# One expert weight piece loaded earlier, normalized rows written contiguously, and filler matmuls ahead of a mixer, in a two-block mixture-of-experts kernel

## The chip, the cores and the metric

The kernel runs on one core of one Trainium2 chip. The metric is the device time of one execution in microseconds (us); less is better. TensorE is called PE, its weight loads PEld, VectorE DVE, ScalarE ACT, GpSimd POOL, and SyncE, whose queue issues nearly all weight transfers, SP.

## What is computed

256 tokens of width 1024 in float32 pass two blocks. The first has two layers, each a mixer (three kinds of attention over one projection) and a mixture of 16 experts, with a layer norm behind each of the two. The second block has another mixer and again 16 experts. Cut to the part around the change:

```python
def first_block(x, ...):
    h = layer_norm(x, ln_in_g, ln_in_b)
    for l in range(DEPTH):                                      # DEPTH = 2
        mix = mixer_sublayer(h, ...)
        h = layer_norm(DEEPNORM_ALPHA * h + mix, ln1_g[l], ln1_b[l])
        ffn = grouped_moe(h, router_w, router_bias, exp_w_gate[l], exp_w_up[l], exp_w_down[l])
        h = layer_norm(DEEPNORM_ALPHA * h + ffn, ln2_g[l], ln2_b[l])
    return h

def grouped_moe(h, ...):                                        # two experts of one group for each token
    ...
    for e in range(N_EXPERTS):                                  # 16
        a = jax.nn.silu(h @ w_gate[e]) * (h @ w_up[e])          # 1024 -> 512
        y = y + dense_gates[:, e:e + 1] * (a @ w_down[e])       # 512 -> 1024
    return y
```

Each expert has 6 MB of weights, so each of the three expert stages reads 96 MB.

## The kernel before

The program is one straight sequence for each engine, with the order of the work written out by hand. Tokens lie in two tiles of 128 partitions (i = 0, 1).

**Experts.** `moe()` treats the 16 experts as 8 pairs. `gather(q)` (L986) brings the tokens of four experts into groups of 64 slots with one-hot matmuls. For each pair, `expand(pr, 0)` and `expand(pr, 1)` (L1026) do gate and up, 32 matmuls each, into one PSUM tile apiece; each of these matmuls needs one 512-wide row of one expert's weight half. `shrink(pr - 1)` (L1073) does the down product of the pair before, `slots` and `turn` (L1042, L1057) prepare the next step, and `scatter(pr - 1)` (L1099, L1101) adds the result into `yacc`. Behind the first gather, PE and the other engines load a flag and branch over `overflow` (L1127, L1128), code for experts with more than 64 tokens which isn't entered with these inputs.

**Weight stream.** `moe_loads` makes a list of 96 jobs of 1 MB for each expert stage: pair 0 gate, pair 0 up, pair 1 gate, pair 1 up, pair 0 down, pair 2 gate and so on, four jobs each (two halves by two experts). A letter in `MOE_SEQ` says from which pool of tiles a job takes its place; job 3, the second half of expert 1's gate in pair 0, has the letter q, four quarter pieces of 256 KB in tiles of the pool "m2" (5 slots), which the mixer before uses for its softmax work. `wload` (L114) issues a job on SP's queue, in order, so a transfer whose tile isn't free yet holds all behind it. `LATE = (3, 21), (3, 20)` takes job 3 out of the list and puts it back at position 21 in the first block's stages and 20 in the second block's: it is issued behind jobs 16 to 19 (pair 0's down) and two or one of pair 2's gate. The mixer issues the first jobs, and `load(MOE_FIRST[blk])` (L1014) those up to 22 or 21. Tiles that the mixer frees late, such as those that PE reads for pada, and the DMA of an ada row, hold some of these jobs.

**From experts to mixer.** The last pair's `scatter` calls `last(i, n)` for each token tile and half: DVE takes statistics of the half row, and after the second half `ln_scale` (L277, on POOL) gives scale and shift and `ln_rest` applies them through `ln_apply` and `evac` (L132 on ACT, L141 on DVE), two instructions for each token tile. They write `xn2` as [token, 8, 128] with the feature index split so that an instruction reads `yacc` with a step of 32 bytes. `to_T` (L291) then transposes each 128x128 block of `xn2` on PE, with the block as the stationary operand, and evacuates it as `h2T` with gain and shift, four pieces on ACT and four on DVE for each tile. Between the two, PE does the `pada` products of an adaptive scale (L1244), 16 matmuls. `warm(n)` (L121) issues n matmuls on a constant that nobody reads.

Of the kernel before, what the change touches and what calls it, by code (L numbers as in the profile page):

```python
# [21 lines left out]
D = 1024  # L22
P = 128
# [8 lines left out]
AHEAD = 6  # L32
KMC, FLG = (1, 3), 3
EXT, EXT2 = 0, 0
LATE = (3, 21), (3, 20)
PARTS = {"r": "rr", "x": "r4", "y": "44", "z": "422", "q": "2222"}
GATHER = (1, 3, 5)
MOE_FIRST = 22, 21
# [2 lines left out]
LNE, ADA_AT, ADA_1 = "p", "ak0", (2, 3)  # L41
# [6 lines left out]
class Net:  # L48
# [1790 lines left out]
    def run(self):  # L1839
        A, nc = self.A, self.nc  # L1840
        self.loads()
        c = self.c
        W = self.mixer_loads(0)
        nc.scalar.preload_act_table_set("silu_and_others")
        hT, hp = self.ln_in()
        for l in range(2):
            nc.gpsimd.tensor_scalar(c["qg", l], c["qg", l], 96 ** -0.5, None, op0=ALU.mult)
        self.wstream([(n, W[n]) for n in WSTREAM])
        self.wahead(2)
        tr = iter(())  # L1850
        for l in range(2):
            fill = self.ada(ADA_MX[l], W["ada"])
            h1 = []
            g, b = c["ln1_g", l], c["ln1_b", l]
            pr, parts = [], []

            def mid(xn):

                h1.append(self.big([P, 8, S], "h1T"))
                self.to_T(xn[:, 0], h1[0], g, b, 0)  # L1860
                self.warm(2)
                parts.append(self.parts())
                self.split_hi(xn, parts[0], 0)
                pr.append(self.ps("prt", "o"))
                self.router_mm(h1[0], c["rw"], 16, pr[0], 0)
                self.warm(3)

            We = lambda e: (A["exp_w_gate"][l, e], A["exp_w_up"][l, e], A["exp_w_down"][l, e])
            loads = self.moe_loads(We, MOE_SEQ[0], LATE[0])
            xn = self.mixer(l, hT, hp, W, fill, mid, tr, loads[0])  # L1870
            h1T, pr, parts = h1[0], pr[0], parts[0]
            self.split_lo(xn, parts, 0)
            self.split_hi(xn, parts, 1)
            self.to_T(xn[:, 1], h1T, g, b, 1)
            yacc = self.big([P, 2, D], "yacc")
            self.to_tok(h1T, yacc[:, 0, :], 0, ALPHA, "a", "s")
            self.warm(2)
            self.router_mm(h1T, c["rw"], 16, pr, 1)
            self.split_lo(xn, parts, 1)
            self.dbg(f"h1T{l}", h1T)  # L1880
            mask, gates = self.router1(pr)

            self.to_tok(h1T, yacc[:, 1, :], 1, ALPHA, "a", "s")
            next(fill, None)
            self.warm(4)
            xn2, sts = [], []

            def last(i, n):
                if i == 0 and n == 0:
                    xn2.append(self.big([P, 2, 8, P], "xn2"))  # L1890
                if n == 0:
                    sts.append(self.stats())
                nc.vector.bn_stats(sts[i][:, n, :], yacc[:, i, n * 512:(n + 1) * 512])
                if n == 1:
                    self.ln_rest(yacc, i, self.ln_scale(sts[i], LNE), xn2[0], "aa" if i == 0 else "av")

            self.moe(0, loads, parts, g, b, mask, gates, We, yacc, None, last, fill)
            Wa = self.ada_loads(ADA_TR[l:l + 1])
            W = self.mixer_loads(1) if l == 0 else self.mixer2_loads()
            fill = self.ada(ADA_TR[l:l + 1], Wa, "s", l == 0)  # L1900
            hT = self.big([P, 8, S], "h2T")
            next(fill)
            if l == 0:
                hp = self.hparts()
                self.wstream([(n, W[n]) for n in WSTREAM])
                for i in range(2):
                    self.to_T(xn2[0][:, i], hT, c["ln2_g", l], c["ln2_b", l], i, "ta"[i])
                next(fill)
                for i in range(2):
                    self.hl_tile(hT, hp, i)  # L1910
                tr = fill
                self.wahead(2)
            else:
                sq = self.big([P, 8, S], "sq2")
                self.wstream([(n, W[n]) for n, _ in WIN2_TILES])
                for i in range(2):
                    self.to_T(xn2[0][:, i], hT, c["ln2_g", l], c["ln2_b", l], i, "ta"[i])
                    self.square2(hT, sq, i)
                hp = self.hparts()
                self.wahead(2)  # L1920
                self.rms2(hT, sq, hp, fill)
        We = lambda e: (A["w1_2"][0, e], A["w3_2"][0, e], A["w2_2"][0, e])
        loads = self.moe_loads(We, MOE_SEQ[1], LATE[1])
        xt, parts, h3T, pr, g2b = self.mixer2(hT, hp, W, loads[0])
        self.dbg("x1", xt)
        self.dbg("h3T", h3T)
        mask, gates = self.router2(pr)

        def last(i, n):
            s = slice(n * 512, (n + 1) * 512)  # L1930
            nc.sync.dma_start(self.out[0, i * P:(i + 1) * P, s], xt[:, i, s])

        self.moe(1, loads, parts, self.mcol[:, 4, :], self.mcol[:, 3, :], mask, gates, We, xt, g2b, last)


# [148 lines left out]
```

## Time and profile before

| | us |
|---|---|
| median of 3 runs | 1238.4 (1237.06 to 1243.48) |
| profiled execution | 1240.28 |
| its span in the trace | 1238.6 |
| PE busy | 1161.9 (94%) |
| mean granted clock of PE | 0.976 |

The three expert stages run from about 191 to 404 (layer 0), 579 to 790 (layer 1) and 1024 to the end (second block), with the mixers between. Times in rows are in us from the start of the span unless ns is said. A row of a timeline gives a group of like instructions on one engine: start, length from the first to the last, engine, line of the kernel, operation, output and inputs, shapes and count, and in brackets the idle time of the engine ahead of it and what ended that. A table by stretches gives, for each stretch, how long each engine was busy, the granted clock of PE (1.00 is its full 2.4 GHz), the busy share of the 16 DMA engines and what they moved.

### The profile page before, as it was taken

Reading aid. Unit: us, or ns where it says so; the run is one execution under the profiler, and the core shown is the slowest. Engines: PE = TensorE matmul, PEld = TensorE weight load, DVE = VectorE, ACT = ScalarE, POOL = GpSimd, SP = SyncE. Lnnn points to the kernel's source line nnn. Section 1 sums busy time; section 2 is a strip of 40 time slices with the busy share of each in tenths; the row PEclk is TensorE's granted clock in tenths of the full one; section 3 lists DMA queues with packets and bytes.
Section 4 is the critical chain, followed back from the end, with each engine's and each line's share of the span. In section 5 each row is a group of like instructions: output and inputs, shape, how many; then the busy total and the mean of one; then the engine's idle time right before and its main releaser. Section 6 shows DMA issues by size and latency. Waiting matters only on the chain. (4 is left out here: it accounts for less than half of the span.)

```text
span 1238.6 us, 16671 instructions
## 1 busy us (share of the span) xinstructions
PE 1161.9 (94%) x6366; PEld 673.6 (54%) x6366; DVE 517.1 (42%) x1135; ACT 381.4 (31%) x799; POOL 245.6 (20%) x356
## 2 busy tenths in 40 slices
PE   5999897999999799997999999899899989999997
PEld 4887453434344688645344343489898453434432
DVE  6565351212232756535023221565985360223323
ACT  5545341111111655424011011465464340101100
POOL 4655200000000356320000000132473200000000
PEclk9999898999999999999999999889899998999999
DMA  9814958999999964677999999984354267999995
GB/s 383 338 65 186 399 185 327 408 404 413 414 416 414 419 256 138 248 263 295 378 405 415 413 415 414 418 321 154 114 194 172 102 263 312 415 414 416 415 417 232
DMA packets 77947, 395.46 MB, mean 319 GB/s; under 512 B 7936, under 2 KB 9592, under 8 KB 49440
## 3 DMA queue, kind: packets, MB, share of 16 engines
q1 hardware_dynamic: 73488, 384.66, 78.2%
q0 software_dynamic: 2608, 7.73, 1.6%
q10 hardware_dynamic: 1760, 1.89, 0.5%
q8 instruction: 53, 0.87, 0.3%
q14 instruction: 38, 0.31, 0.1%
HBM read 389.41 MB, written 6.51 MB: 320 GB/s over the span
## 5 line engine op out<-in xcount | busy, mean ns | idle before, releaser
L1026 PE MATMUL pz<-we,xT 128*64 128x512 f32 x1536 | 343.9, 604 | 19.8 <-DMA we<-in_exp_w_gate 12.3
L1026 PEld LDWEIGHTS pz<-we,xT 128*64 128x64 f32 x1536 | 110.8, 139 | 239.6 <-issue 217.8
L1073 PE MATMUL py<-wd,aT 128*64 128x512 f32 x768 | 171.1, 593 | 0.9 <-DMA wd<-in_w 0.9
L1035 DVE TENSOR_TENSOR act<-sil,pz 128x512 f32<-128x512 f32 x24 | 16.5, 688 | 327.8 <-PE pz L1026 302.8
L1050 POOL TENSOR_SCALAR m_ge<-m_s 64x1 f32<-64x1 f32 x48 | 11.9, 247 | 586.5 <-DVE m_s L1045 339.9
L1073 PEld LDWEIGHTS py<-wd,aT 128*64 128x64 f32 x768 | 56.6, 137 | 110.2 <-issue 105.6
L1030 ACT ACTIVATE sil<-pz 128x512 f32<-128x512 f32 x24 | 14.3, 597 | 217.8 <-PE pz L1026 217.8
L1079 ACT ACTIVATE yh<-py,m_ge 128x512 fp32r<-128x512 f32 x32 | 22.0, 688 | 187.6 <-PE py L1073 187.6
L1080 DVE SCALAR_TENSOR_TENSOR yl<-py,m_ge,yh 128x512 fp32r<-128x512 f32 x32 | 24.0, 751 | 96.3 <-ACT yh L1079 96.3
L541 PE MATMUL pout<-w_o,oT 128*128 128x512 f32 x128 | 58.2, 602 | 0.0
L986 PE MATMUL pg<-G,xhi 128*128 128x256 f32 x192 | 47.8, 290 | 2.0 <-DVE G L975 2.0
L448 POOL TENSOR_SCALAR E<-E,r 128x128 f32<-128x128 f32 x40 | 31.6, 791 | 77.4 <-DVE r L444 77.2
L986 PE MATMUL pg<-G,xlo 128*128 128x256 f32 x192 | 46.7, 283 | 0.0
L1085 ACT ACTIVATE yh<-yf 128x512 fp32r<-128x512 f32 x16 | 10.1, 631 | 104.0 <-DVE yf L1084 104.0
L1099 PE MATMUL psc<-yh,GT 128*128 128x512 f32 x96 | 39.3, 410 | 1.1 <-ACT yh L1085 0.8
L1101 DVE TENSOR_TENSOR yacc<-yacc,psc 128x512 f32<-128x512 f32 x64 | 40.1, 680 | 0.0
L1099 PE MATMUL psc<-yl,GT 128*128 128x512 f32 x96 | 38.5, 401 | 1.3 <-DVE yl L1080 0.6
L541 PEld LDWEIGHTS pout<-w_o,oT 128*128 128x128 f32 x128 | 23.8, 194 | 26.0 <-issue 25.6
L986 PEld LDWEIGHTS pg<-G,xhi 128*128 128x128 f32 x192 | 36.7, 191 | 2.4 <-issue 1.6
L986 PEld LDWEIGHTS pg<-G,xlo 128*128 128x128 f32 x192 | 36.8, 191 | 0.0
L442 ACT ACTIVATE E<-s,nm 128x128 f32<-128x128 f32 (+1 forms) x48 | 20.2, 421 | 47.9 <-DVE nm L441 45.6
L1244 PE MATMUL pada<-wa,cz 128*32 128x512 f32 x192 | 24.2, 618 | 8.4 <-DVE yacc L1101 4.5
(512 smaller groups left out, 2122.4 us busy)
## 6 DMA issues: line engine op xcount, KB each, us to landing
wd<-in_exp_w_down SPq DMA_DIRECT2D x58, 1024.0 KB, 16.3
we<-in_exp_w_up SPq DMA_DIRECT2D x54, 1024.0 KB, 13.1
we<-in_w SPq DMA_DIRECT2D x52, 1024.0 KB, 15.0
we<-in_exp_w_gate SPq DMA_DIRECT2D x48, 1024.0 KB, 11.7
wd<-in_w SPq DMA_DIRECT2D x29, 1024.0 KB, 15.3
wa<-in_p_ada SPq DMA_DIRECT2D x24, 1024.0 KB, 15.2
we<-in_exp_w_gate SPq DMA_DIRECT2D x28, 512.0 KB, 13.7
we<-in_w SPq DMA_DIRECT2D x22, 512.0 KB, 14.8
```

The source lines that it names most:

```text
L442: nc.scalar.activation(E[:, s], sc[:, s], AF.Exp, bias=nm[:, i:i + 1], accum_out=sm[:, i:i + 1])
L448: self.nc.gpsimd.tensor_scalar(E[:, 0:P], E[:, 0:P], r[:, 0:1], None, op0=ALU.mult)
L541: self.nc.tensor.matmul(acc, oT[:, cc, i * P:(i + 1) * P], w[cc][:, n * 512:(n + 1) * 512], start=(cc == 0), stop=(cc == 7), skip_group_ch ...
L986: nc.tensor.matmul(pg[:, :256], part[:, i, k, :], Gq[q][:, i].rearrange("p e s -> p (e s)"), start=(n == 0), stop=(n == 3))
L1026: nc.tensor.matmul(pz[64 * e:64 * e + 64, :], x[:, k, o + 64 * e:o + 64 * e + 64], w[e][k], start=(k == 0), stop=(k == 7), skip_group_chec ...
L1035: nc.vector.tensor_mul(a, st[pr].pop("sil"), pz)
L1073: nc.tensor.matmul(py[n][64 * e:64 * e + 64, :], aT[:, f, 64 * e:64 * e + 64], w[e][f][:, n * 512:(n + 1) * 512], start=(f == 0), stop=(f ...
L1079: nc.scalar.activation(yh[:, s], py[n], AF.Copy, scale=ge)
L1080: nc.vector.scalar_tensor_tensor(yl[:, s], py[n], ge, yh[:, s].bitcast(F32), op0=ALU.mult, op1=ALU.subtract)
L1099: nc.tensor.matmul(pt, GT[:, i * P:(i + 1) * P], y[:, s], start=(j == 0), stop=(j == 1), skip_group_check=True)
L1101: nc.vector.tensor_tensor(yacc[:, i, s], yacc[:, i, s], pt, op=ALU.add)
L1244: nc.tensor.matmul(pa[32 * k:32 * k + 32, :], c["cz"][:, 4 * k4 + k:4 * k4 + k + 1].to_broadcast([P, 32]), w[:, k, :], start=(k4 == 0), st ...
```

## The change

Three edits. Job 3 is put back at position 16 of the list in all three expert stages, that is right behind job 16 and ahead of jobs 17 to 21 (17 to 20 in the second block). `xn2` becomes [token, tile, 1024] and is written contiguously, tile 0 by ACT, tile 1 by ACT and DVE; `to_T` gets a rearranged view of it, so that the transposes' stationary operand is read with a step of 32 bytes. And `warm(9)` and `warm(4)` are put around the first `next(fill)` behind the experts (the pada matmuls), in both layers.

```diff
-LATE = (3, 21), (3, 20)
+LATE = (3, 16), (3, 16)
...
             def last(i, n):
                 if i == 0 and n == 0:
-                    xn2.append(self.big([P, 2, 8, P], "xn2"))
+                    xn2.append(self.big([P, 2, D], "xn2"))
...
                 if n == 1:
-                    self.ln_rest(yacc, i, self.ln_scale(sts[i], LNE), xn2[0], "aa" if i == 0 else "av")
+                    rs, nm = self.ln_scale(sts[i], LNE)
+                    for j in range(2):
+                        s = slice(j * 512, (j + 1) * 512)
+                        self.evac(xn2[0][:, i, s], yacc[:, i, s], rs, nm, "a" if i == 0 else "av"[j])
...
             hT = self.big([P, 8, S], "h2T")
+            self.warm(9, "t")
             next(fill)
+            self.warm(4, "t")
             if l == 0:
...
                 for i in range(2):
-                    self.to_T(xn2[0][:, i], hT, c["ln2_g", l], c["ln2_b", l], i, "ta"[i])
+                    self.to_T(xn2[0][:, i].rearrange("t (q k) -> t k q", k=8), hT, c["ln2_g", l], c["ln2_b", l], i, "ta"[i])
...
                 for i in range(2):
-                    self.to_T(xn2[0][:, i], hT, c["ln2_g", l], c["ln2_b", l], i, "ta"[i])
+                    self.to_T(xn2[0][:, i].rearrange("t (q k) -> t k q", k=8), hT, c["ln2_g", l], c["ln2_b", l], i, "ta"[i])
                     self.square2(hT, sq, i)
```

## Rows read from the trace of the kernel before

**Rows 1.** Table by stretches: length, engines' busy time, PEclk, DMA share, GB/s
```profile
176.20:191.00 14.80, 13.78 (x100) 11.14 (x99) 9.33 (x32) 9.36 (x15) 2.11 (x4) 0.88 0.77 287
191.00:230.00 39.00, 31.99 (x137) 10.70 (x137) 3.24 (x12) 3.45 (x5) 0.87 (x3) 0.91 0.96 365
230.00:386.00 156.00, 156.00 (x783) 66.79 (x780) 39.48 (x76) 23.18 (x37) 3.60 (x13) 1.00 1.02 413
564.00:578.50 14.50, 12.51 (x100) 9.58 (x99) 10.55 (x38) 10.21 (x17) 1.48 (x3) 1.00 0.79 294
578.50:614.00 35.50, 28.96 (x124) 9.99 (x126) 2.39 (x9) 2.26 (x4) 0.88 (x3) 0.90 0.96 376
1024.00:1035.00 11.00, 11.00 (x40) 3.72 (x42) 0.00 (x0) 0.60 (x1) 0.00 (x0) 0.74 0.46 157
```

**Rows 2.** DMA issues at 365.8: transfer, count, size, us to landing
```profile
wd<-in_exp_w_down SPq DMA_DIRECT2D x1, 1024.0 KB, 20.1
```

**Rows 3.** Timeline of PE, pair 6's down product in layer 0
```profile
383.73 7.59 PE L1073 MATMUL py<-wd,aT 128*64 128x512 f32 x32
```

**Rows 4.** Timeline of PE, pair 0 in layers 0 and 1, an undisturbed pair
```profile
191.59 4.50 PE L1026 MATMUL pz<-we,xT 128*64 128x512 f32 x18 [0.35 <-ACTq L1128]
202.47 12.79 PE L1026 MATMUL pz<-we,xT 128*64 128x512 f32 x46 [6.38 <-DMA we<-in_exp_w_gate]
578.78 4.48 PE L1026 MATMUL pz<-we,xT 128*64 128x512 f32 x18 [1.23 <-PEq L1128]
589.22 12.27 PE L1026 MATMUL pz<-we,xT 128*64 128x512 f32 x46 [5.97 <-DMA we<-in_exp_w_gate]
1197.16 13.95 PE L1026 MATMUL pz<-we,xT 128*64 128x512 f32 x64
```

**Rows 5.** Timeline of SP's queue around layer 0's first expert pair
```profile
176.61 14.29 SPq L114 DMA_DIRECT2D wd<-in_exp_w_down  x4
191.00 6.18 SPq L114 DMA_DIRECT2D we<-in_exp_w_gate  x8
```

**Rows 6.** Waits of SP's queue, 170 to 226: releaser, total us, times, longest
```profile
SPq L114 <- PE pada L1244: 6.4, 1, 6.4
SPq L114 <- DMA ada<-wa: 6.1, 1, 6.1
```

**Rows 7.** Timeline of PE, head of the second block's experts
```profile
1010.49 2.57 PE L121 MATMUL warm<-onesb 128*128 128x512 bf16 x11
1023.91 16.81 PE L1026 MATMUL pz<-we,xT 128*64 128x512 f32 x64 [5.52 <-issue]
```

**Rows 8.** DMA queues, 609.2 to 1022.6: packets, MB, share
```profile
q8 instruction: 18, 0.29, 0.3%
```

**Rows 9.** Table by stretches, 609 to 1021.4 and the last gather
```profile
608.97:1021.36 412.39, 392.99 (x2286) 251.68 (x2282) 195.84 (x405) 147.17 (x284) 86.61 (x101) 0.98 0.75 295
1013.80:1018.50 4.70, 4.20 (x32) 3.95 (x32) 2.60 (x8) 2.24 (x4) 0.50 (x1) 1.00 1.03 410
```

**Rows 10.** DMA queues, 1021.3 to 1022.6: packets, MB, share
```profile
q8 instruction: 1, 0.02, 5.3%
```

**Rows 11.** Timelines of PE and ACT behind the experts of layers 0 and 1
```profile
406.49 1.92 PE L1244 MATMUL pada<-wa,cz 128*32 128x512 f32 x16 [2.23 <-DVE yacc L1101]
406.88 2.55 ACT L132 ACTIVATE xn<-yacc,nm,rs 128x512 f32<-128x512 f32 x2 [4.90 <-POOL nm L277]
409.49 1.09 PE L291 MATMUL pt<-pk,xn 128*128 128x128 f32 x8 [1.07 <-ACT xn L132]
409.86 1.33 ACT L132 ACTIVATE xn<-yacc,nm,rs 128x512 f32<-128x512 f32 x1 [0.42 <-POOL nm L277]
411.09 2.88 ACT L132 ACTIVATE h2T<-pt,pk 128x128 f32<-128x128 f32 x8
799.88 5.99 PE L1327 MATMUL pss<-sq,ones 128*128 128x128 f32 x32 [0.76 <-ACT sq L1315]
```

**Rows 12.** The page, costliest groups: busy us, mean ns, idle before; contiguous write on ACT
```profile
L1085 ACT ACTIVATE yh<-yf 128x512 fp32r<-128x512 f32 x16 | 10.1, 631 | 104.0 <-DVE yf L1084 104.0
```

## Prediction of the time after the change

> **What bounds the kernel now.** The page gives TensorE (PE) as busy nearly throughout, which doesn't say what a saved microsecond of PE is worth, so I read the table by stretches first, then the last jobs of the stages, then their heads. In the steady part of the first expert stage (230 to 386) PE is busy without a gap at full clock, and the DMA engines move 413 GB/s with their share at its top [rows 1]: the two run level. Which of them ends the stage is seen at its last jobs. The down half of pair 6 is issued at 365.8 and lands 20.1 us later, at 385.9 [rows 2], while pair 6's down product, which uses it, starts at 383.73 and takes 7.59 us [rows 3]; the run is stretched because it caught up with its weights. So PE has little slack before the weight stream, and **an expert stage ends earlier only by the DMA time that is recovered**, not by all the PE time.
>
> At the head of a stage both have holes. In layers 0 and 1 PE does 18 of the 64 matmuls of pair 0's gate and up, then waits 6.38 and 5.97 us for the gate's fourth piece; the other 46 take 12.79 and 12.27 us, where an undisturbed pair takes 13.95 for 64 (0.218 each, 10.0 for 46): the granted clock fell behind the wait (means of 0.91 and 0.90 there [rows 1]) and cost 2.8 and 2.2 us more [rows 4]. The piece is issued late: SP's queue issues four down jobs from 176.61 to 190.9, held by pada for 6.4 us and by an ada row for 6.1 us, and only behind them the gate's transfers from 191.00 [rows 5, 6]. The DMA engines have spare time meanwhile. At 413 GB/s, 176.2 to 191 moved 287 (14.8 x (1 - 287/413) = 4.5 us idle) and 191 to 230 moved 365 (4.5 us); in layer 1, 564 to 578.5 moved 294 (4.2) and 578.5 to 614 moved 376 (3.2) [rows 1].
>
> **Edit 1, the piece ahead of the down jobs.** It adds and removes no byte; four 256 KB transfers pass jobs 17 to 21 (17 to 20 in the second block) on SP's queue. Issuing them costs SP under 0.8 us each (eight transfers in 6.18 us, waits included [rows 5]), and SP waits 6.4 us for pada right behind them anyway [rows 6]. Their tiles' slots were last used by the mixer's softmax work and ought to be free by then. In layer 0 the piece then goes at about 177 and lands before 190, the 6.4 us wait goes, and the clock should hold. PE's part: 6.4 + 2.8 = 9.2 us, in layer 1 6.0 + 2.2 = 8.2, and perhaps the 1.23 us at the branch. DMA's part: 1.05 MB more move in the first stretch, 1.05/0.413 = 2.5 us of its 4.5. Two us stay there, since the down jobs behind it still wait for pada and the ada row, which don't move [rows 6]. Of the 4.5 behind 191, pair 0's earlier end frees the next buffers about 9 us sooner, and 2.7 to 4.5 come back. Together 5.2 to 7.0; I take **6.0**. Layer 1 likewise 2.5 + 2.0 to 3.2 = 4.5 to 5.7; I take **5.3**. The rest of PE's saved 9 us should turn into small waits for down tiles near the stage's end.
>
> The second block differs. Its fourth piece isn't what PE waits for: PE idles 5.52 us until 1023.91 with nothing named as releaser ("issue"), and then runs all 64 matmuls in 16.81 us [rows 7], 2.9 us over 13.95, in a stretch with mean clock 0.74 where DMA fell to 157 GB/s (11 x (1 - 157/413) = **6.8 us idle**) [rows 1]. The idle PE lies just behind the gather and the branch over the overflow code. Instruction packets on queue q8 are rare: 18 between 609 and 1022.6 [rows 8], for 2286 matmuls and 2282 weight loads [rows 9], 254 instructions to a packet. The last of them moves inside this idle time, after 1021.3 [rows 10]. I read it as PE waiting for the code behind the branch. The fillers of edit 3 put 26 matmuls and weight loads, 52 instructions, ahead of this place (26 for each layer), so the place where a packet is wanted falls 52 instructions earlier; the gather ahead of the branch is 64 instructions in 4.2 us [rows 9], so the packet is wanted up to 52/64 x 4.2 = 3.4 us earlier, and PE would start near 1020. Only then could the fourth piece, issued behind the down jobs here too, have bound, and edit 1 has moved it away. If so PE gains about 3.9 us at the start and 2.9 of clock, and DMA's hole closes: 6.0 to 6.8, I take **6.0**. If the packet comes as late as before, **0**. Nothing in the trace of before tells me at which instruction a packet is asked for, so both ends stay in the range.
>
> The Trainium skill, "Runtime: NRT & Kernel Launch", section "Instruction fetch mechanics", says that engines' code streams in 16 KiB blocks of 256 instructions and that a taken branch to a target that isn't loaded waits for a DMA fetch. The 254 instructions to a packet agree with it; that the wait depends on where the branch falls in a block follows from the rule, but no run of before shows it moved.
>
> **Edit 2, normalized rows written as they lie.** Each of four rows per layer (two token tiles by two halves) is written contiguously. ACT's row with the 32-byte step took 1.33 and 1.27 us [rows 11]; a contiguous 128x512 on ACT took 0.631 [rows 12]. Tile 0's two rows end 1.3 us earlier, tile 1's 0.7. PE's chain: transposes of tile 0 at 409.49 waited 1.07 for them, those of tile 1 follow the 1.33 us row, and then eight evacuations of 2.88 us set the mixer's start [rows 11]. These aren't shortened, and they begin with tile 1's row done: gain 0.6 in layer 0. In layer 1 the same 0.5, with a clock that falls there too: 32 matmuls of the square sums take 5.99 us, 0.19 each [rows 11]. If the new fillers hold the clock, up to 2.1 more; together I take **1.5** in layer 1, **0.6** in layer 0.
>
> In exchange the transposes take their stationary operand with the 32-byte step. No PE operand of before has that step, so its price is bounded: 0 by PE's own pace (8 in 1.09 us [rows 11]), and at the other end ACT's pace at this step, 1.33 us/512 = 2.6 ns a column, 0.33 us for 128, 2.7 us for 8: 1.6 more per tile. Tile 0's has 1.1 us in hand while ACT writes tile 1's row, tile 1's has none: 2.1 us per layer, 4.2 in all at most. A gain is excluded, since the same 128 columns are read. I take 0, because the evacuations behind them, at 0.36 us a piece, are still slower than ACT's pace per transpose (0.33), so the chain goes on at its old rate. The Trainium skill, "SBUF — State Buffer", section "Door 1: The DMA port swizzle", says that accesses that go to a new 16-byte line each time pay a penalty. ACT's 1.33 against 0.631 agrees; by it the transposes would be slower, which is rival D.
>
> **Edit 3, fillers.** 9 + 4 matmuls of 0.234 us (11 took 2.57) [rows 7]. Nine are 2.1 us against the 2.23 us in which PE waits ahead of pada; four are 0.9 and end by about 409.4, where the transposes start at 409.49 [rows 11]. Cost 0 while that cover stands; up to 0.5 us per layer as edit 2 lets the transposes start 1 us sooner, which is in the 0.6 above.
>
> **The sum.** 6.0 + 5.3 + 6.0 + 0.6 + 1.5 = 19.4 us. The profiled execution took 1240.28 us (span 1238.6), 1.9 above the median 1238.4. From it 1220.9, from the median 1219.0; I say 1220.
>
> **Rivals and chances.** About 0.5% (6.2 us) is what a measurement of this kernel tells from no change.
> A, as summed, 1220: 0.42.
> B, the packet of the second block comes as late as before: without the 6.0, 1226: 0.23. For it: the delay may be the branch's, not the block's.
> C, PE's time passes whole (buffers free earlier carry the stream on): 9.2 + 8.2 + 6.8 + 2.1 + 1.2 = 27.5, 1211: 0.10. Against it: the shrink that caught up [rows 3].
> D, the strided transposes cost their 4.2: 1224 with A, 1230 with B: 0.10. For it: ACT's two rows [rows 11, 12]; against it: ACT's evacuations set the pace.
> E, waits for the late down tiles become long enough for the clock to fall again, as behind the waits for the piece [rows 4], 2 to 3 us per layer on top of B: 1231: 0.06.
> F, slower: the piece's tile slots aren't free at 177. SP issues in order, so 17 to 21 then wait behind the piece. From the point at which the slots come free later than the transfers issued by then have landed (I put it at 184), the engines run dry, and where they come only at 191, up to 5 us per layer: 10, less the 2 us of edit 2: 1247: 0.05. For it: the trace shows that the slots were free at 191, not at 177.
> G, nothing gained, the stages end by the same last transfers: 1237: 0.04.
> Faster by over 0.5%: A to D and most of E, 0.88; within: the rest of E, G and a mild F, 0.08; slower: F, 0.04. The range leaves out F, G and the far end of C: 1212 to 1231.
>
> **What would show it.** Right: pair 0's 64 matmuls in one run of about 14 us in layers 0 and 1, SP issuing the piece ahead of 178; over 380 GB/s from 176 to 230 but for the pada wait; a PE start in the second block within 2 us of the branch, and no fall to 157 GB/s. Wrong: a wait of several us at pair 6's down product, an "issue" wait of 5 us at the second block's start, transposes above 1.1 us per 8 in both transitions, or down jobs issued later than before.

## The result: 12 to 14 us faster, and the profile after

The changed kernel takes 1225.47 us (median of 4 runs, 1222.1 to 1226.33) against 1237.83 us of the kernel before (4 runs). The ratio is 0.9883, with a 95% interval of 0.9852 to 0.9913. Run again beside the later experiments it took 1226.28 us (6 runs, 1223.07 to 1227.08) against 1240.66, a ratio of 0.9879 (0.9854 to 0.9904). The forecast was 1220 us with a range of 1212 to 1231: the direction and the range hold, the gain is two thirds to four fifths of the 18.4 us forecast.

The profiled execution took 1224.84 us, span 1223.2 (before: 1240.28 and 1238.6). Where its 15.4 us come from is read off PE's timeline. A stage is counted from the first gather matmul's start to the last scatter's end, the mixers lie between; negative numbers are time saved.

| stretch | before | after | difference | forecast |
|---|---|---|---|---|
| up to the first gather | 187.1 | 185.6 | -1.6 | 0 |
| experts of layer 0 | 217.1 | 211.6 | -5.5 | -6.0 |
| mixer of layer 1 | 169.2 | 170.3 | +1.1 | -0.6 |
| experts of layer 1 | 216.9 | 212.9 | -4.0 | -5.3 |
| second block's mixer | 223.8 | 222.6 | -1.3 | -1.5 |
| experts of the second block, tail included | 224.4 | 220.2 | -4.2 | -6.0 |

In the profile of the repeat the three stages came out the same (-5.6, -4.0, -4.0); the first line did not (-0.1). No edit lies ahead of that point, so it isn't part of the change: of that time PE had its lower clock for 10.2 us in the first profile of the changed kernel, and for 17.1 us in the profile of before and in that of the repeat.

The heads of the stages, from PE's timeline of the changed kernel (start, length, engine, line, operation, tiles, shapes, count, idle time ahead and its releaser), to be held against [rows 4, 7]:

```profile
192.42 13.95 PE L1026 MATMUL pz<-we,xT 128*64 128x512 f32 x64 [2.74 <-PEq L1128]
573.70 15.60 PE L1026 MATMUL pz<-we,xT 128*64 128x512 f32 x64 [2.10 <-PEq L1128]
1010.21 15.65 PE L1026 MATMUL pz<-we,xT 128*64 128x512 f32 x64 [3.04 <-PEq L1128]
```

The waits of 6.38 and 5.97 us for the gate's piece are gone, and pair 0's matmuls stand in one run. In layer 0 they take the 13.95 us of an undisturbed pair; in layer 1 and the second block the granted clock fell in them (15.60 and 15.65 us). What's new is the bracket: PE now waits 2.74 us in layer 0 and 2.10 in layer 1 at its own branch, where it had 0.35 and 1.23.

SP's queue, to be held against [rows 5]: the four quarter pieces go out at 175.72, the down jobs behind them are held as before.

```profile
175.19 0.42 SPq L114 DMA_DIRECT2D wd<-in_exp_w_down  x1
175.72 2.23 SPq L114 DMA_DIRECT2D we<-in_exp_w_gate  x4
178.04 12.28 SPq L114 DMA_DIRECT2D wd<-in_exp_w_down  x3
```

The table by stretches (length, busy time of PE, PEld, DVE, ACT, POOL, granted clock, DMA share, GB/s) is to be held against [rows 1]; the stretches are the same pieces of work, moved with it:

```profile
174.60:189.40 14.80, 13.77 (x101) 10.87 (x99) 9.52 (x32) 9.50 (x16) 2.12 (x4) 0.90 0.93 337
189.40:221.00 31.60, 28.56 (x137) 10.91 (x137) 3.24 (x12) 3.48 (x5) 0.87 (x3) 1.00 0.99 395
558.00:572.50 14.50, 12.57 (x101) 9.57 (x99) 10.57 (x37) 10.23 (x17) 1.48 (x3) 1.00 0.92 338
572.50:602.00 29.50, 27.99 (x126) 10.13 (x128) 2.41 (x9) 2.32 (x4) 0.88 (x3) 0.94 1.00 401
1010.00:1021.00 11.00, 10.79 (x44) 4.28 (x46) 0.52 (x4) 1.13 (x2) 0.25 (x1) 0.84 0.81 301
```

By the prediction's own arithmetic (length x (1 - GB/s over 413)) the DMA engines' idle time in these stretches is 2.7 + 1.4 us in layer 0 (before 4.5 + 4.5), 2.6 + 0.9 in layer 1 (before 4.2 + 3.2) and 3.0 in the second block (before 6.8). Recovered are 4.9, 3.9 and 3.8 us; the stages got 5.5, 4.0 and 4.2 us shorter. **The stages gained what the DMA engines recovered, within 0.6 us.** By itself this is bookkeeping, since the same bytes at the same full rate take less time by as much as the idle time shrinks, whichever engine waited for the other. What tells the limit is PE: pair 0 got 9.7 and 7.1 us shorter in layers 0 and 1 (first to last start), and with the new wait at the branch counted, pair 1's gate starts 7.4 and 6.2 us sooner behind the first gather, more than the stages gained. Where the rest went is seen at pair 6's down product, layer 0, to be held against [rows 3]:

```profile
374.85 2.74 PE L1073 MATMUL py<-wd,aT 128*64 128x512 f32 x10
378.93 5.36 PE L1073 MATMUL py<-wd,aT 128*64 128x512 f32 x22 [1.34 <-DMA wd<-in_exp_w_down]
```

It starts 8.9 us sooner than before (7.3 us, counted from the first gather), and waits for its down tile. From its first to its last start it takes 8.9 us, where before had 7.0 and the pairs ahead of it have 6.4: the 7.4 us are 5.5 us of gain and 1.9 of waiting. In layer 1 the 6.2 us are 4.0 and 2.2 (9.1 us against 6.9).

### The profile page after: what moved, and what is told of

It reads as the page before. It is cut to its first block, busy times and chain, and to the rows that moved or that the text cites. A ratio compares the mean times of both kernels' runs of the same rounds, so it can differ in the third digit from the quotient of the medians.

```text
span 1223.2 us, 16729 instructions
## 1 busy us (share of the span) xinstructions
PE 1159.0 (95%) x6392; PEld 670.9 (55%) x6392; DVE 515.9 (42%) x1135; ACT 377.8 (31%) x799; POOL 245.7 (20%) x356
## 5 line engine op out<-in xcount | busy, mean ns | idle before, releaser
L1026 PE MATMUL pz<-we,xT 128*64 128x512 f32 x1536 | 338.2, 598 | 8.2 <-PEq L1128 7.9
L1026 PEld LDWEIGHTS pz<-we,xT 128*64 128x64 f32 x1536 | 111.4, 138 | 221.7 <-issue 210.4
```

The lines of the kernel that those rows point to most:

```text
L1026: nc.tensor.matmul(pz[64 * e:64 * e + 64, :], x[:, k, o + 64 * e:o + 64 * e + 64], w[e][k], start=(k == 0), stop=(k == 7), skip_group_chec ...
```

## Experiments

Two theories are at stake. **Stream**: a stage ends when its weights have come, so that only recovered DMA time counts; its rival is that the stage is as long as PE's work and waits. **Packet**: PE's wait behind the branch is for a packet of code that is asked for at a fixed instruction, so that 52 instructions of fillers moved it; its rival is that the wait belongs to the branch. Stage lengths below are from one profiled execution of each kernel; of the lengths, the repeat of the changed kernel differs by at most 0.2 us, but clock falls differ between executions and are named where they matter.

| kernel | layer 0 | layer 1 | second block | last gather to first gate start | median us |
|---|---|---|---|---|---|
| before | 217.1 | 216.9 | 220.1 | 0.6, 1.5, 5.8 | 1238 to 1241 |
| after | 211.6 | 212.9 | 215.9 | 3.0, 2.4, 3.3 | 1225.5 |
| late_only | 211.8 | 210.7 | 219.4 | 3.0, 2.7, 5.7 | 1227.7 |
| fill_only | 217.7 | 216.6 | 216.5 | 0.6, 1.4, 3.0 | 1234.9 |
| norm_only | 218.7 | 217.4 | 219.2 | 1.3, 1.5, 5.6 | 1237.2 |
| before_shift64 | 219.2 | 218.1 | 216.3 | 0.6, 0.5, 3.0 | 1237.0 (one) |
| after_shift64 | 211.6 | 212.1 | 217.0 | 0.6, 0.5, 3.0 | 1223.4 |
| after_keep20 | 212.9 | 212.8 | 216.9 | 3.2, 2.3, 3.6 | 1224.5 |
| shift64_pe12 | 211.9 | 211.4 | 216.6 | 0.6, 0.5, 3.0 | 1225.8 (one) |
| after_swap | 210.5 | 211.6 | 216.8 | 2.8, 2.6, 3.0 | 1225.4 |
| after_swap_shift64 | 210.0 | 211.3 | 214.6 | 0.6, 0.5, 3.0 | 1221.1 |
| swap_shift64_join | 210.6 | 213.5 | 216.1 | 0.6, 0.5, 3.0 | 1223.1 |
| swap_shift64_fill2 | 210.4 | 211.1 | 214.4 | 0.6, 0.5, 3.0 | 1219.0 |

### Each edit alone

```diff
-LATE = (3, 21), (3, 20)
+LATE = (3, 16), (3, 16)
```

> Edit 1 alone (job 3 at position 16 in all stages), no contiguous rows, no fillers. Measured for all three edits, from the first gather to the last scatter of a stage: 5.5 us shorter in layer 0, 4.0 in layer 1, 4.2 in the second block. Theory 'packet' (PE waits behind the branch for a code packet that is asked for at a fixed instruction, so the fillers' 26 matmuls and weight loads, 52 instructions, moved it): layer 0 as with all edits, 5.5 shorter; layer 1, whose packet is asked for 26 instructions later than with all edits, 2.5 to 4.0 shorter; second block within 1 us of before, with an idle PE of over 5 us behind the branch. Whole: 8 to 10 us faster than before. Rival 'branch' (the wait belongs to the branch and not to the place of the code): second block 4 us shorter as with all edits, whole 13 us faster. Rival 'edit 1 gives nothing to the stage's end': all three stages within 1 us of before.

1227.7 us (1226.49 to 1228.65, ratio 0.9916, 0.9899 to 0.9934), 10.5 us faster. Layer 0 gained 5.3 us as with all edits, the second block 0.7, and its wait is back, at the same place as before:

```profile
1011.28 15.61 PE L1026 MATMUL pz<-we,xT 128*64 128x512 f32 x64 [5.45 <-PEq L1128]
```

So the second block's gain was not edit 1's. Layer 1 is a miss: 6.3 us shorter where 2.5 to 4.0 were expected. Over the stretch from 12 us ahead of the gather to 8 us ahead of the last down product the DMA engines moved 82.93 MB here and 83.77 MB in the changed kernel, at 405 GB/s both: 0.84 MB more were already there, 2.0 us at 413 GB/s. The mixer ahead was 0.3 us longer than the changed kernel's, so this execution reached the gather with more of the stream behind it. Its pair 0 in layer 1 also ran without the clock fall that the changed kernel has there (13.4 us from first to last start against 15.0); after_shift64, without the fall too and with 83.69 MB, has 212.1 us, so the fall is worth at most 0.8 of the 2.2. A stage's length by itself is uncertain by that much.

```diff
+            self.warm(9, "t")
             next(fill)
+            self.warm(4, "t")
```

> Edit 3 alone (9 + 4 filler matmuls behind the experts of layers 0 and 1). Theory 'packet': in the second block PE starts 2 to 3.5 us sooner behind the branch (idle 2 to 3.5 us where before had 5.5) and then waits 1 to 3 us for the gate's late fourth piece, stage 1 to 3 us shorter; layers 0 and 1 within 0.5 us of before. Rival 'branch': idle PE of 5.5 us as before, stage unchanged. If the fillers hold the clock behind layer 1's experts, that mixer is 1 to 2 us shorter; if they don't, within 0.5. Whole: 2 to 4 us faster by 'packet', 0 to 2 by 'branch'.

1234.87 us (10 runs, ratio 0.9974, 0.996 to 0.9988). Of 3.3 us, the second block's stage gave 3.6 in the profile, by a start 2.8 us sooner, more than the 1 to 3 expected; layers 0 and 1 moved by +0.5 and -0.3.

```profile
1018.85 15.34 PE L1026 MATMUL pz<-we,xT 128*64 128x512 f32 x64 [2.72 <-ACTq L1128]
```

Packet holds against branch. But the expected wait for the gate's piece is absent: all 64 matmuls stand in one run with the piece at its old place 20. And the new bracket names ACT's queue at the branch: 3.0 us behind the last gather's start, another limit stands.

```diff
-                    self.ln_rest(yacc, i, self.ln_scale(sts[i], LNE), xn2[0], "aa" if i == 0 else "av")
+                    rs, nm = self.ln_scale(sts[i], LNE)
+                    for j in range(2):
+                        s = slice(j * 512, (j + 1) * 512)
+                        self.evac(xn2[0][:, i, s], yacc[:, i, s], rs, nm, "a" if i == 0 else "av"[j])
```

(with the new shape of `xn2` and the rearranged view in `to_T`)

> Edit 2 alone (rows written contiguously, transposes with the 32-byte step). Theory: 0.5 to 0.7 us less between the last scatter and the first matmul of the next mixer in both layers, the expert stages within 0.5 us of before, whole 1 us faster. Rival 'transposes pay': eight transposes take 2 us and more instead of 1.1 in each of two tiles, whole 0 to 3 us slower.

1237.15 us (10 runs, ratio 0.9983, 0.9971 to 0.9995). Between the stages of layers 0 and 1 it took 168.6 us instead of 169.2: 0.6 less, as expected. PE's transposes and ACT's rows, against [rows 11]:

```profile
408.57 1.16 PE L291 MATMUL pt<-pk,xn 128*128 128x128 f32 x8
410.85 1.16 PE L291 MATMUL pt<-pk,xn 128*128 128x128 f32 x8 [1.11 <-ACT xn L132]
407.00 1.52 ACT L132 ACTIVATE xn<-yacc,nm,rs 128x512 f32<-128x512 f32 x2 [4.89 <-POOL nm L277]
409.98 0.81 ACT L132 ACTIVATE xn<-yacc,nm,rs 128x512 f32<-128x512 f32 x1 [1.46 <-POOL nm L277]
```

Tile 0's two rows take 1.52 us instead of 2.55, and ACT then waits 1.46 us for tile 1's scale, which POOL sends no sooner: of tile 0's gain nothing passes on. Eight transposes take 1.16 us, not 1.09; the rival is out. The second block's mixer was 1.8 us shorter, of which more below. The stages of layers 0 and 1 were 1.6 and 0.5 us longer, against the expectation; no instruction in them is altered. What differs is their head, in layer 0 to be held against [rows 4]:

```profile
190.76 4.48 PE L1026 MATMUL pz<-we,xT 128*64 128x512 f32 x18 [0.99 <-PEq L1128]
201.96 13.37 PE L1026 MATMUL pz<-we,xT 128*64 128x512 f32 x46 [6.73 <-DMA we<-in_exp_w_gate]
```

Pair 1's gate starts 1.5 and 0.5 us later behind the gather than before. In the four kernels without edit 1 (before, fill_only, norm_only, before_shift64) the lengths of these two stages follow that start within 0.2 us, over 2.3 us in layer 0 and 1.5 in layer 1. There PE's time at the head counts whole; only behind edit 1 does the stream take part of it back.

### Where the code lies

```diff
+        ps = self.ps("nudge", "a")
+        for _ in range(32):
+            nc.tensor.matmul(ps[:, 0:16], c["onesb"], c["oneb"].to_broadcast([P, 16]), start=True, stop=True,
+                             skip_group_check=True)
         W = self.mixer_loads(0)
```

> The changed kernel with 32 small matmuls (16 columns each, read by nobody) on PE ahead of the first layer norm, where PE is idle until 8.8 us: 64 instructions more ahead of all that follows, nothing else. Theory 'packet': each stage's packet is asked for 64 instructions sooner, the waits behind the branch (2.74, 2.10 and 3.04 us in the changed kernel) fall below 1 us in all three stages; what the stream makes of it is 0.5 to 1.4 us in layer 0, 0.5 to 0.9 in layer 1, 2 to 3 in the second block: whole 3 to 5 us faster than the changed kernel. Rival 'branch': waits and time as in the changed kernel, within 1 us.

> The kernel before with the 64 small instructions on PE at the program's start, and none of the three edits. Theory 'packet': the second block's idle PE behind the branch falls from 5.8 to about 3.0 us (the wait for ACT that stood behind it), its stage is 2.5 to 3.6 us shorter; layers 0 and 1 within 0.5 us, since there the gate's fourth piece is what PE waits for. Rival 'the fillers act by themselves, as warm-up or by their place': no change in the second block.

In the changed kernel, 32 small matmuls and their 32 weight loads 180 us ahead of the place take the wait away:

```profile
190.06 13.95 PE L1026 MATMUL pz<-we,xT 128*64 128x512 f32 x64 [0.35 <-ACTq L1128]
570.22 13.95 PE L1026 MATMUL pz<-we,xT 128*64 128x512 f32 x64 [0.23 <-ACTq L1128]
1006.83 15.42 PE L1026 MATMUL pz<-we,xT 128*64 128x512 f32 x64 [2.73 <-ACTq L1128]
```

The packet itself shows it. In the changed kernel one moves in the 1.3 us from 189.6, just behind the gather; with the 64 instructions one moves in the microsecond from 185, at the gather's start (185.6). The lines are those of queue q8 in these two stretches, packets, MB, share:

```profile
q8 instruction: 1, 0.02, 4.9%
```

```profile
q8 instruction: 1, 0.02, 5.5%
```

All traces bear it out. Wherever PE waits at the branch with its own queue (or "issue") named, it starts 2.5 to 2.9 us after a packet of q8 has begun to move: packet and start are 1021.36 and 1023.91 in the second block of before, and 189.72 and 192.42, 571.01 and 573.70, 1007.44 and 1010.21 in the changed kernel. Where the packet began earlier than that, PE has no such wait. The shift isn't exact, though: in layer 1 the 26 instructions of fill_only moved the packet by 0.1 us against the gather, and 64 moved it by 3.5.

In the kernel before, without any of the edits, the same 64 instructions take the second block's stage from 220.1 to 216.3 us, its first row there being

```profile
1021.98 15.32 PE L1026 MATMUL pz<-we,xT 128*64 128x512 f32 x64 [2.73 <-ACTq L1128]
```

Its layers 0 and 1, expected within 0.5 us, were 2.1 and 1.2 us longer, with waits of 7.98 and 8.29 us for the gate's piece instead of 6.38 and 5.97; pair 1's gate starts 2.3 and 1.1 us later behind the gather, and as in norm_only that passes whole.

**Packet is shown**: it needs no fillers at the place, no edit of the work, only instructions somewhere ahead. It has a limit that the expectation of after_shift64 missed: in the second block the next wait, for ACT at the branch, stood 0.3 us behind the one removed, so of the 2 to 3 us expected there nothing came (217.0 us against 215.9, with a clock fall in pair 0 in both). The whole, 1223.39 us (1222.38 to 1223.68), is 2.1 us below the changed kernel's median, less than the 3 to 5 expected, and its runs overlap.

For the stream theory the first line is the telling one: PE starts 2.4 us sooner behind the gather in layer 0, and the stage's length is 211.6 us with and without it. Pair 6's down product gave all of it back, in waits:

```profile
372.52 1.02 PE L1073 MATMUL py<-wd,aT 128*64 128x512 f32 x2
373.86 1.93 PE L1073 MATMUL py<-wd,aT 128*64 128x512 f32 x6 [0.32 <-DMA wd<-in_exp_w_down]
376.42 1.07 PE L1073 MATMUL py<-wd,aT 128*64 128x512 f32 x2 [0.63 <-DMA wd<-in_exp_w_down]
378.97 5.36 PE L1073 MATMUL py<-wd,aT 128*64 128x512 f32 x22 [1.48 <-DMA wd<-in_exp_w_down]
```

### Edit 1 in the second block

```diff
-LATE = (3, 16), (3, 16)
+LATE = (3, 16), (3, 20)
```

> The changed kernel with job 3 left at position 20 in the second block (edit 1 in layers 0 and 1 only). Theory 'packet': what shortened the second block's stage (4.2 us with all edits, 3.6 with the fillers alone, 0.7 with edit 1 alone) is the code's place; PE doesn't wait for the piece there even at position 20: stage within 0.7 us of the changed kernel, no wait for the gate's piece. Rival (the prediction's step): with PE started sooner, the piece at position 20 binds: a wait for it of 1 to 3 us in pair 0's gate, stage 1 to 3 us longer.

```profile
1010.32 15.65 PE L1026 MATMUL pz<-we,xT 128*64 128x512 f32 x64 [3.28 <-PEq L1128]
```

1224.46 us (6 runs) beside 1226.28 of the changed kernel in the same batch. There is no wait for the piece; the second block's stage is 216.9 us against 215.9 and 216.1. (Layer 0's, 212.9 us, began 1.2 us sooner than the changed kernel's and ends at the same time, 397.3 against 397.2.) Edit 1 in the second block is worth at most the 0.7 to 1.0 us that this and late_only show, and the medians don't show it at all.

The changed kernel ran once more beside it, unaltered:

> The changed kernel unaltered, as the mark for the others of this batch: 1222 to 1226.5.

1226.28 us, as told above.

### PE's time against the stream

```diff
(after_shift64, and at the end of each pair's turn in moe())
+            if pr == 3:
+                self.warm(12, "t")
```

> As after_shift64, with 12 filler matmuls (2.8 us of PE time by 0.234 each) behind pair 3 in each of the three stages. In after_shift64 pair 6's down product took 11.2 and 11.8 us in layers 0 and 1, where 7.0 is its undisturbed length, so PE has 4 us in hand there. Theory 'stream': the stages of layers 0 and 1 keep their length within 0.5 us, pair 6's down product is 2.5 to 3 us shorter; in the second block (8.5 us, 1.4 in hand) the stage is 1 to 2 us longer. Rival 'PE': all three stages 2.8 us longer, whole 8 us slower than after_shift64.

```profile
285.99 2.79 PE L121 MATMUL warm<-onesb 128*128 128x512 bf16 x12
377.21 2.74 PE L1073 MATMUL py<-wd,aT 128*64 128x512 f32 x10
381.29 5.36 PE L1073 MATMUL py<-wd,aT 128*64 128x512 f32 x22 [1.35 <-DMA wd<-in_exp_w_down]
```

2.79 us of useless PE work in each stage changed the stages by +0.3, -0.8 and -0.4 us. The waits at pair 6's down product took most of it: first to last start 8.9, 8.4 and 6.4 us instead of 11.2, 11.8 and 8.5. (6.4 is what the pairs ahead of it take; the 7.0 that the expectation calls undisturbed is pair 6 of before, stretched by 0.6.) **Stream is shown** in layers 0 and 1. In the second block, against the 1 to 2 us expected, work added in mid-stage passes too. (The single time, 1225.79 us, is 3.4 us above after_shift64's profiled one: 2.1 us lie ahead of the first gather and 1.7 in layer 1's mixer, where the clock fell; the stages together are 0.9 shorter.)

### More DMA time recovered

```diff
             jobs.insert(late[1], jobs.pop(late[0]))
+            if SEQ == MOE_SEQ[0]:
+                jobs[18:22] = jobs[20:22] + jobs[18:20]
```

> The changed kernel with jobs 20 and 21 (pair 2's gate, first two) put ahead of jobs 18 and 19 on SP's queue in layers 0 and 1, since 18 and 19 hold the queue until pada and the ada row are through, while the DMA engines idle for 3.0 and 3.4 us in the 12 us ahead of the first gather of the stages. Theory 'stream' (a stage ends earlier by the DMA time that is recovered): if the two jobs' tiles are free by then, 2 to 3 us less DMA idle time in each of the two stages, stages 2 to 3 us shorter, pair 6's wait for its down tile shorter by as much, whole 4 to 6 us faster than the changed kernel. Rival 'PE' (the stage is as long as PE's work and its own waits at the stage's head): the head is as before, stages within 0.5 us. Where the tiles aren't free, no theory sees a difference.

> The two jobs ahead of 18 and 19 as in after_swap, and the 64 small instructions on PE at the program's start as in after_shift64. Theory 'stream': the instructions alone took PE's wait behind the branch away in layer 0 (2.4 us) and shortened the stage by 0.0, because DMA was the limit; with 2 to 3 us of DMA time recovered, the stages are 2 to 3.5 us shorter than with either alone in layers 0 and 1: whole about 1218 to 1220 us. Rival 'PE': as after_shift64, 1223.

after_swap took 1225.43 us, no different from the changed kernel's 1225.47. In its profile the stages are 1.1 and 1.4 us shorter in layers 0 and 1, not 2 to 3, and the second block's mixer and stage, which the edit doesn't touch, 0.9 us longer each. The tiles were free, and the DMA engines had no hole left behind the gather, but the hole ahead of it stayed. With the 64 instructions as well it took 1221.11 us (1219.82 to 1221.84), layers 0 and 1 1.7 and 0.8 us shorter than in after_shift64. That is the direction of the stream theory, at half the size expected. The table by stretches of after_swap_shift64 says where the rest is: ahead of 188 DMA still moves 327 GB/s, behind it it runs full.

```profile
175.00:188.00 13.00, 11.97 (x84) 8.84 (x82) 8.50 (x31) 8.27 (x13) 2.11 (x4) 0.87 0.90 327
188.00:200.00 12.00, 11.66 (x65) 5.42 (x65) 2.64 (x10) 3.58 (x5) 0.25 (x1) 1.00 1.02 409
200.00:220.00 20.00, 19.68 (x96) 6.94 (x94) 1.79 (x5) 1.19 (x2) 0.62 (x2) 1.00 1.01 415
```

In the second block, where the order of the jobs is the same in both, after_swap_shift64's stage is 2.4 us shorter than after_shift64's (214.6 against 217.0). PE starts at the same point, but in the first pair 0 runs at full clock and in the second it doesn't (15.42 us), and the DMA engines follow. The 15 us from the gather on, after_swap_shift64 first:

```profile
1006.59 13.95 PE L1028 MATMUL pz<-we,xT 128*64 128x512 f32 x64 [2.73 <-ACTq L1130]
999.67:1014.67 15.00, 12.27 (x70) 6.72 (x72) 4.67 (x20) 4.58 (x8) 0.36 (x2) 1.00 0.99 382
999.91:1014.91 15.00, 12.27 (x64) 6.60 (x66) 4.67 (x20) 3.98 (x7) 0.36 (x2) 0.89 0.88 336
```

So PE's time in pair 0 does count in the second block: while the DMA engines still have idle time at the head, a faster PE recovers it.

```diff
(after_swap_shift64, and in moe())
-        nc.scalar.preload_act_table_set("silu_and_others")
 ...
         self.overflow(parts, g, b, W, flag, gov, yacc, colscale, *lend())
+        nc.scalar.preload_act_table_set("silu_and_others")
```

> As after_swap_shift64, and ACT's load of the table for Silu (1.28 us) moved behind the branch over the overflow code. With the code packet there in time, PE still waits 2.73 us at the branch of the second block, put down to ACT's queue at the branch. Theory 'the branch is a meeting of all engines, ACT comes last': PE starts up to 1.3 us sooner in the second block, its stage 0.5 to 1.3 us shorter. Rival (ACT comes to the branch without waiting for its table load, or DVE's and POOL's gate work is the last): no change there, within 0.5 us.

1223.11 us (1221.02 to 1224.0); the wait for ACT at the second block's branch is still 2.7 us. The table load isn't what ACT comes late by. The trace of after_shift64 shows what stands ahead of the branch in ACT's order: two steps of the second block's gates, in turn with DVE's, the last of which ends at 1006.17, 2.1 us behind the gather's end; PE starts at 1006.83. In layers 0 and 1 ACT has no such steps there. No run moved them.

```profile
1005.94 0.23 ACT L1822 ACTIVATE r_s<-r_s 128x32 f32<-128x32 f32 x1 [0.74 <-DVE r_s L1821]
```

```diff
(after_swap_shift64, and in moe())
         gather(0)
+        if blk == 1:
+            self.warm(8, "o")
```

> As after_swap_shift64, and 8 filler matmuls (1.9 us) behind the first gather of the second block, in the 2.73 us in which PE waits there for ACT at the branch. Theory: the wait is not longer, and the clock doesn't fall behind it; where it fell (13.36 us without, 14.8 to 15.1 with a fall for pair 0's 64 matmuls from first to last start), that stage is 1.5 to 2 us shorter. after_swap_shift64's profile had no fall there by itself, so its stage (214.6 us) is the mark: 214 to 215. Whole 1219 to 1221. Rival 'the fillers delay the branch': 0.5 to 2 us longer.

```profile
1002.70 1.92 PE L121 MATMUL warm<-onesb 128*128 128x512 bf16 x8
1005.61 13.95 PE L1030 MATMUL pz<-we,xT 128*64 128x512 f32 x64 [0.99 <-ACTq L1132]
```

1219.0 us (5 runs, 1215.53 to 1219.35), a ratio of 0.982 (0.9792 to 0.9848) to before, and 7.3 us below the changed kernel in the same batch: the fastest version run. The start isn't later, and pair 0 runs at full clock (13.95 us against 15.65). after_swap_shift64 had no fall there either in its profile, so that the fillers hold the clock isn't shown; by stage the two are alike (214.4 and 214.6).

## Why the prediction was right, and where its terms were off

**The bound was right.** "An expert stage ends earlier only by the DMA time that is recovered" is what after_shift64 and shift64_pe12 show from both sides for layers 0 and 1 with edit 1 in. In the kernel before the two were level, as the prediction says: pair 6's run was stretched by 0.6 us (7.0 against 6.4 from first to last start), PE had no other wait from pair 1 to pair 6, and its time at the head counted whole until it met the stream, for 5.5 of 7.4 and 4.0 of 6.2 us. The waits that were forecast "near the stage's end" stand at pair 6's down product [rows 3]. Rival C, which let all of PE's time pass, is out by that.

**Edit 1 in layers 0 and 1.** The 6.0 us were 5.5 (5.6 in the repeat), inside 5.2 to 7.0. The 5.3 were 4.0 in both profiles, below the 4.5 to 5.7: of the 4.2 us of DMA idle time ahead of 578.5 only 1.6 came back instead of 2.5, though the piece filled its 2.5 us. The remaining 2.6 and 2.7 us ahead of the gather are those of the down jobs held for pada and the ada row [rows 6], put at 2. The clock, whose 2.2 us in layer 1 the sum counted as regained, fell in pair 0 there in both profiles; with the clock up and the wait at the branch gone, in after_shift64, the stage gained 4.8, inside the range. late_only's 6.3 shows that a single stage's length can't be held to better than 2 us. No step foresaw the packet of code coming late in layers 0 and 1, where it cost PE 2.4 and 0.9 us; it cost the stage nothing in layer 0, where PE wasn't the limit (211.6 us without it too), and at most 0.8 in layer 1 (212.1 against 212.9).

**The second block.** That the packet's place decides, and that the fillers move it, was right; before_shift64 shows it by itself. Rival B's cause is out. The term of 6.0 us measured 4.2 and 4.0. Two of its numbers were too large. PE was to start 3.9 us sooner, 1.6 us behind the gather's end, though the step's own shift comes to 3.4 at most; it started 2.5 sooner, 3.04 behind it. The packet began to move 4.5 us behind the gather's start instead of 7.2, and an earlier one wouldn't have helped much, since ACT holds PE until 2.7 us behind the gather's end. The packet's wait stood in front of that, but ACT's last step ahead of the branch (L1822, 1020.23 to 1020.46) is in the trace of before. And the clock was to stay up, but fell still behind the shorter wait (15.65 us for 64 matmuls against 13.95), so 1.2 of 2.9 us came back. Where it did stay up, in after_swap_shift64 and swap_shift64_fill2, the stage is 5.5 and 5.7 us shorter than before, near the 6.0. One statement was wrong: that with PE started sooner "the fourth piece, issued behind the down jobs here too," could have bound. In fill_only and after_keep20 PE starts sooner with the piece at place 20 and doesn't wait for it.

**Edit 2.** 0.6 us in layer 0 is what norm_only has. It comes from tile 1's row alone, as the step had it. The price of the strided transposes was taken as 0 and is 0.07 us per eight; rival D is out. (The sign that stood for it, transposes "above 1.1 us per 8 in both transitions", did come, with 1.16 for tile 1's eight in both.) The weight loads of the transposes show the step's cost: 193 ns each in the changed kernel, 140 before, by the views of PEld by shapes of this stretch.

```profile
L291 PEld LDWEIGHTS pt<-pk,xn 128*128 128x128 f32 x16 | 2.0, 193 | 0.8 <-ACT xn L132 0.6
L291 PEld LDWEIGHTS pt<-pk,xn 128*128 128x128 f32 x16 | 1.7, 140 | 2.9 <-ACT xn L132 2.9
```

So the rule of the Trainium skill that the prediction set against this edit ("SBUF — State Buffer", section "Door 1: The DMA port swizzle": accesses that go to a new 16-byte line each time pay a penalty) agrees with the trace. It is a penalty of 1.4 times, and PE's own pace hides it. The prediction took 2.1 times for ACT from two different instructions [rows 11, 12]; the same instruction of ACT went from 1.33 to 0.81 us, 1.6 times.

**The transitions as a whole** came out otherwise than the sum says. Layer 1's mixer was 1.1 us longer, in the repeat too (170.3). The chain gained its half microsecond; then the granted clock fell to its lower level, 1.2 GHz, at the mixer's first matmuls, behind a wait of 1.62 us for `h2T` (table by stretches, same columns as above; a mean of 0.53):

```profile
406.40:410.00 3.60, 3.54 (x9) 2.88 (x10) 2.21 (x3) 3.60 (x8) 2.62 (x3) 0.53 1.02 426
```

The same fall is in the repeat, after_keep20 and shift64_pe12 and isn't in fill_only, norm_only, after_shift64 or the four swap kernels, whose mixers took 168.6 to 169.1 us (late_only and before_shift64 have falls at other places). norm_only has the same wait, 1.63 us, without the fall, so the wait alone doesn't set it off; what does is open.

The 1.5 us forecast for the other transition were 1.3, in part by luck. Edit 2's half microsecond is there: in all profiles with it the square sums [rows 11] start 9.0 us behind the stage's end, in those without it 9.5. They end 15.5 us behind it in before and 13.6 in the changed kernel, so the clock that fell in them before and held now gave 1.4 more. But it held in late_only and before_shift64 too (14.2 us), which have neither edit 2 nor the fillers; that the fillers hold it is not shown. The rest of the mixer was 0.6 us longer, on unchanged work.

**The other rivals.** F is out: SP issues the piece at 175.72 without a wait, and the down jobs behind it at 178.04. E's waits are there, but the 22 matmuls behind the 1.34 us take 5.36 us, at most 0.25 each, so the clock didn't fall behind it. G is out. The sum of the five terms, 19.4 us, measured 13.9 in the first profile (5.5 + 4.0 + 4.2 + 1.3 - 1.1): 0.5, 1.3 and 1.8 us less than forecast in the stages and 0.2 and 1.7 in the transitions. Clock falls that the sum had counted as regained, or hadn't counted, lie behind most of it; the rest of that profile's 15.4 lies ahead of the first gather, on unchanged work. The two comparisons of medians give 12.4 and 14.4. That the measured 1225.5 is the time of rival B (1226) is chance: the packet did come sooner, and B's 6.0 us were lost in smaller parts elsewhere.

## What to carry to other kernels

Where an engine and the weight stream run level, read the DMA engines' idle time by stretches and count only as much of the engine's saved time as can recover it; a wait of 6 us on the engine that was removed here was worth 4 to 5.5, and its remainder reappears as waits on the stream's last tiles. A wait marked "issue" or with the engine's own queue just behind a branch can be for code: a few dozen instructions anywhere ahead move it, so an edit that adds instructions can win or lose microseconds in a place that it doesn't touch, and edits should be timed alone before the gain is credited. Behind a removed wait, look for the next engine at the same meeting point; its last step ahead of that point can stand in the trace of before, as ACT's did here.

## What the runs showed of the hardware

- A packet of code can come later where no code ahead of it has changed. In layer 0, without the 64 instructions, it began to move 1.3 to 2.3 us behind the gather's start in the kernels without edit 1 and 3.9 to 4.4 in those with it, and PE's wait at the branch was 0.35 to 0.99 us and 2.49 to 2.96. With edit 1 the DMA engines were busier in this stretch (a share of 0.93 against 0.77 [rows 1]), but that their load delays the packet is not shown: in the second block edit 1 didn't delay it (6.9 us in late_only, 7.2 before). The Trainium skill, "Runtime: NRT & Kernel Launch", section "Instruction fetch mechanics", has blocks of 256 instructions fetched by DMA and a wait where a taken branch leaves the loaded ones. The packets of 16 KB and the wait for one just behind the branch agree, and the runs add a size: PE starts 2.5 to 2.9 us after the packet begins to move.
- In the same transposes, a weight load of 128 columns of float32 read with a step of 32 bytes took 193 ns, a contiguous one 140.
- The granted clock fell at places that differ between executions of one kernel and kernels of equal work: 15.65 us instead of 13.95 for 64 matmuls behind one of them, more than edit 2 is worth in all.
